# Half of the memory's keys computed inside the gated scan, its weights in joint chunks, and other due times for the side work, in a two-layer hybrid decoder trunk

## The chip, the cores and the metric

The kernel runs on one core of one Trainium2 chip. The metric is the device time of one execution in microseconds (us): 1093.5 us before the change, the median of three runs (1093.49, 1093.5 and 1094.94).

The core has five engines that matter here: PE (TensorE) multiplies matrices, DVE (VectorE) and ACT (ScalarE) work elementwise, POOL (GpSimd) does a few elementwise operations, and SP (SyncE) issues the transfers. Each runs its own list of instructions in order, and a semaphore holds an instruction back until what it reads is there.

## The reference, cut to what matters

Two layers are applied to 256 tokens of 1024 features, all in float32:

```python
for l in range(2):
    h = rmsnorm(x, norm_mix[l])
    u_ssm, q_lat, kv_lat, k_rope, hg_q, hg_f, hg_i, hg_g, gate_logits = split(h @ w_in[l])
    # s5_mixer: a scan over complex states, then a gated product
    y = gelu(s5_scan(u_ssm))                      # (256, 512)
    z_out, z_gate = split(y @ ssm_w_glu[l], 2)    # (512, 2048) weights
    y_ssm = z_out * sigmoid(z_gate)
    y_mla = mla_mixer(...)                        # 8 heads of causal attention, @ mla_w_o
    y_hg  = hgrn2_mixer(...)                      # gated linear recurrence, @ hg_w_o
    g = sigmoid(gate_logits).reshape(1, 256, 3, 1024)
    merged = g[:, :, 0] * y_ssm + g[:, :, 1] * y_mla + g[:, :, 2] * y_hg
    x = x + merged @ w_out[l]
    # memory cross-attention, 4 heads of 128, over 256 memory rows
    mem_n = rmsnorm(mem, norm_mem[l])
    k, v = split(mem_n @ x_w_kv[l], 2)            # the keys and values of the memory
    q = rmsnorm(x, norm_cross[l]) @ x_w_q[l]
    x = x + softmax(q @ k.T / sqrt(128)) @ v @ x_w_o[l]
    gt, up = split(rmsnorm(x, norm_ffn[l]) @ ffn_w_gate_up[l], 2)
    x = x + (silu(gt) * up) @ ffn_w_down[l]
return rmsnorm(x, norm_final)
```

The keys `k` need the memory and `x_w_kv` alone, not `x`.

## The kernel before, in words

**Products.** Activations lie feature-major (128 features on the partitions, 256 tokens along them). A float32 product is computed as three products of rounded parts: each operand is a high part H and a low part L, and H·H, H·L and L·H are summed (`mm3`, and three calls of `mm` in `projB`). In the rows of the trace such a triple reads `x2` with `wH` and `x1` with `wL`, or a 128x512 `wH` product and a 128x256 `wL` product.

**Weights.** They stream in as `Chunk`s of up to 1 MB. SP issues one transfer for each source of a chunk, into one of three raw buffers (`RB`); a chunk is cut into `Unit`s of 128x1024, and each unit is split by a copy on ACT (L232, `wH<-raw`) and a subtraction on DVE (L221, `wL<-raw,wH`), with four buffers each (`HU`). `pump` splits up to four units ahead of the product that uses them, and loads three chunks beyond that. The order of the chunks is the order in which `build_chunks` makes them. The weights of the gated scan, `ssm_w_glu`, come as eight chunks of 512 KB a layer (mode "one", a unit each), all others that matter here as 1 MB with two units.

**Stages.** In a layer the order is: the input projections and the products that feed the three mixers; then `ORDER`: gates of HGRN2 (`gh`), gates of the attention (`gm`), the output of HGRN2 (`ho`), gates of the scan (`gs`), the output of the attention (`mo`), and the gated scan (`zo`, the function `scan`, for the two halves i = 0, 1 of the features). `scan` computes the gate `zg` and the output `zo` in four PSUM banks, each in two halves of the contraction; DVE multiplies and adds them into the merged activation (`mu`, `Tg`), PE transposes it (`mT`, L1415), and ACT and DVE split it into H and L (`m`). Then come the product with `w_out` (`quad` for four 128-row tiles, then two times `halves`), `drain()`, the keys of the memory `Kc` in two halves (`hv<-ex`), the norm, the queries (`hv<-h`), and the rest of the cross-attention and the FFN. `ex` is the normalised memory, prepared by a task that `scan(0)` starts and whose normalising factor `Rm` is multiplied in at the end.

**The side work and its order.** The S5 scan, HGRN2, the attention and the preparation of the memory are generators. While PE's gate and projection products are written out, `pace()` steps them on a clock of estimated times: the next step of a task comes due `LATS[layer]` microseconds after the last (0.9 in layer 0, 1.7 in layer 1). `drain()` and `until()` step them to the end. The framework's scheduler then orders each engine's list by readiness and priority (`tc.high_priority`), and `keep_in_program_order` pins an instruction where it was written. There are eight PSUM banks, and SBUF slots that are planned by the tiles' lifetimes.

**S5 in layer 0.** `b<-Ush,G` are 32 products of the scan's input, DVE turns them in about 16 operations (`w`, then `X`) into states, and `y<-Cp,X` are the products of the states that follow. Gate products (`gt`) and pieces of attention (`S`, `PT`, `oT`, with `Ssb` on DVE and ACT) lie between.

**The start.** `first(k)` runs before each k of the first product: it makes `h` and squares `xp`; POOL adds the squares (L659, `sq<-sq,sq`). After the product come the column sums `ms` (two products with a vector of ones), the factor R (`row`, L629: two transposes on PE and a copy on ACT), `Ue<-quad,R` on DVE, and `hg_bounds`, some 15 operations of 128x4 elements on DVE; the scheduler had put most of those between the `wL` of the first product.

Of the kernel before, what the change touches and what calls it, by code (L numbers as in the profile page):

```python
# [9 lines left out]
F32 = mybir.dt.float32  # L10
# [4 lines left out]
ALU = mybir.AluOpType  # L15
# [85 lines left out]
SLOTS = dict(t4=23, t2=10, t1=4, tn=8, tk=8, ps=8)  # L101

LEAD = 2
LATS = (0.9, 1.7)
WIDE = 2
HEADS = 3

# [51 lines left out]
def trunk(ctx, tc, A, out, plan):  # L159
# [32 lines left out]
    def bank(name="acc"):  # L192
        return plan.tile(pp, "ps", [128, 512], F32, nm(name))
# [16 lines left out]
    def mm(o, l, r, start=True, stop=True):  # L210
        n = width(r)
        now["pe"] += max(0.12, 0.451e-3 * n) if l.dtype == F32R else 2 * max(0.112, 0.844e-3 * n)
        return PE.matmul(o, l, r, start=start, stop=stop)  # L213
# [4 lines left out]

    def tt(o, a, b, op):
        dve(o)  # L220
        DVE.tensor_tensor(out=o, in0=a, in1=b, op=op)  # L221

    def ts(o, a, s1, s2=None, o0=ALU.mult, o1=None):
        dve(o, 0.55e-3)
# [145 lines left out]
    def wcols(w, k0, nk, c0, ncol, mode="col", parts=None):  # L370
        return Chunk([wap(w, k0, nk, c0, ncol)], nk, ncol, mode, parts)
# [92 lines left out]
    def wide(w, nk, c0):  # L464

        return [wcols(w, k, min(4, nk - k), c0, 512, "row") for k in range(0, nk, 4)]
# [16 lines left out]
    def build_chunks(l):  # L483
        C = {}
        w = A["w_in"][l]
        C["u"] = [wcols(w, 4 * i, 4, O_U, 512, "row") for i in range(2)]
        for name_, o, n in (("hf", O_HF, 2), ("hq", O_HQ, 2), ("hi", O_HI, 2), ("hg", O_HG, 2), ("ql", O_QL, 2)):
            if name_ == "hi":
                C[name_] = wide(w, 8, o)
            else:  # L490
                C[name_] = [wcols(w, 0, 8, o + 256 * i, 256) for i in range(n)]
        C["kv"] = wcols(w, 0, 8, O_KV, 256)
        C["kr"] = wcols(w, 0, 8, O_KR, 32, "hl")
        C["uq"] = [wcols(A["mla_w_uq"][l], 0, 4, 384 * i, 384, parts=[
            lambda r: r.rearrange("p k (h d) -> p k h d", d=96)[:, :, :, 0:64],
            lambda r: r.rearrange("p k (h d) -> p k h d", d=96)[:, :, :, 64:96]]) for i in range(2)]
        C["ukv"] = wcols(A["mla_w_ukv"][l], 0, 2, 0, 1024, parts=[
            lambda r: r.rearrange("p k (h d) -> p k h d", d=128)[:, :, :, 0:64],
            lambda r: r.rearrange("p k (h d) -> p k h d", d=128)[:, :, :, 64:128]])
        C["gt"] = {}  # L500
        for part in ORDER:
            for i in range(2):
                if part[0] == "g":
                    C["gt"][part[1], i] = wide(w, 8, O_GT + 1024 * "smh".index(part[1]) + 512 * i)
                elif part == "zo":
                    for k in (0, 2):
                        for n, c0 in (("zg", 1024), ("zo", 0)):
                            C[n, i, k] = wcols(A["ssm_w_glu"][l], k, 2, c0 + 512 * i, 512, "one")
                else:
                    C[part, i] = wide(A[dict(ho="hg_w_o", mo="mla_w_o")[part]][l], 4, 512 * i)  # L510
        C["wo"] = [wcols(A["w_out"][l], 4 * i, 4, 0, 512, "row") for i in range(2)]
        C["wo"] += [wcols(A["w_out"][l], 0, 8, 256 * i, 256) for i in range(2, 4)]
        C["xk"] = [wcols(A["x_w_kv"][l], 0, 8, 256 * i, 256) for i in range(2)]
        C["xq"] = [wcols(A["x_w_q"][l], 0, 8, 256 * i, 256) for i in range(2)]
        C["xv"] = wide(A["x_w_kv"][l], 8, 512)
        C["xo"] = [wcols(A["x_w_o"][l], 0, 4, 512 * i, 512, "col" if i else "row") for i in range(2)]
        w = A["ffn_w_gate_up"][l]
        C["gu"] = [[Chunk([wap(w, 4 * i, 4, 0, 256), wap(w, 4 * i, 4, DFF, 256)], 4, 512, "row") for i in range(2)]]
        C["gu"] += [(wcols(w, 0, 8, 256 * i, 256), wcols(w, 0, 8, DFF + 256 * i, 256)) for i in range(1, 11)]
        C["dn"] = [wide(A["ffn_w_down"][l], KF, 0)] if l == L - 1 else []  # L520
        C["dn"] += [[wcols(A["ffn_w_down"][l], k0, nk, 256 * i, 256, "row" if l == L - 1 else "col")
                     for k0, nk in ((0, 8), (8, 8), (16, 6))] for i in range(2 if l == L - 1 else 0, 4)]
        return C
# [50 lines left out]
    def fold(s, E=None):  # L574

        if E is not None:
            E.tensor_tensor(out=s[:, 0], in0=s[:, 0], in1=s[:, 1], op=ALU.add)
        else:
            tt(s[:, 0], s[:, 0], s[:, 1], ALU.add)
        return s[:, 0]  # L580

    def col_sums(s, ps=None):

        ps = ps if ps is not None else bank("ms")[:, 0:2]
        for tt_ in range(2):
            mm(ps[:, tt_:tt_ + 1], s[:, tt_ * 128:tt_ * 128 + 128], ones)
        return ps

    def hidden(name):
# [52 lines left out]
    def first(k):  # L642

        j = k // 2
        if k == 0:

            warm = bank("warm")
            for q in range(WARM):
                PE.matmul(warm[:, 128 * (q % 4):128 * (q % 4) + 128], still, still, start=True, stop=True)
            now["pe"] = 0.0  # L650
        if k % 2 == 0:
            for o in range(2):
                split_g(nrm.x[k + o][:, 0], nrm.x[k + o][:, 1], xk(k + o), gain("norm_mix", k + o))
        else:
            s = t2([2, 256], F32, "sq")
            act(s, xp[j], AF.Square)
            sq0.append(s)
            if j:
                POOL.tensor_tensor(out=sq0[0], in0=sq0[0], in1=s, op=ALU.add)  # L659
            if j == 3:  # L660
                fold(sq0[0], POOL)


    hb = const.tile([128, 2, 2, 4], F32, name="hb")
# [4 lines left out]
    def hg_bounds():  # L669
        lbp = tn([2, 4])  # L670
        lo = off["hg_lb"]
        lmx = tn([4])
        tt(lmx, gcol[:, lo:lo + 4], gcol[:, lo + 4:lo + 8], ALU.max)
        for l in range(2):
            tt(lbp[:, l, :], gcol[:, lo + 4 * l:lo + 4 * l + 4], lmx, ALU.subtract)
        act(lbp, lbp, AF.Exp)
# [509 lines left out]
    def layer(l, nrm):  # L1186
# [20 lines left out]
            return a  # L1207

        qp = quad(C["u"], hx, first if l == 0 else None, 512 if wider else 256)
        if l == 0:  # L1210
            nrm.sums = col_sums(sq0[0][:, 0])
        ms, r = nrm.finish()
        R = const.tile([128, 256], F32, tag="R", name=nm("R"))
        row_of(r, R)
# [174 lines left out]
        def scan(i):  # L1389
            zg, zo = [[bank(n) for _ in range(2)] for n in ("zg", "zo")]  # L1390

            def half(n, ps, k):
                for tt_ in range(2):
                    projB(C[n, i, k], range(2), 0, 512, ps[tt_], yHL, tt_, kbase=k, first=k == 0, last=k == 2)
            half("zg", zg, 0)
            half("zo", zo, 0)
            if i == 0:
# [4 lines left out]
            for tt_ in range(2):  # L1402
# [2 lines left out]
                ts(g_, g_, 0.25, 0.25, ALU.mult, ALU.add)  # L1405
                stt(u2[tt_], u2[tt_], 1.0, g_, ALU.add, ALU.mult)
            half("zo", zo, 2)
            tps = [bank("mT") for _ in range(2)]
            for tt_ in range(2):
                acc = Tg["h", i][:, tt_]  # L1410
# [8 lines left out]
                    k = 4 * i + 2 * q + o  # L1419
                    split(mx_[k][:, 0], mx_[k][:, 1], two(tps[q])[:, o])  # L1420

        ex = []
        for part in ORDER:
            if part == "zo":
                until(yHL)
# [19 lines left out]
            upd(i, halves(C["wo"][i], mx_), 0.5)  # L1445

        drain()
        Kc = t4([4, 256], F32, "Kc")
        Rm = t1([256], F32, "Rm")
        row_of(rmc, Rm)  # L1450
        for i in range(2):
            kc = Kc[:, 2 * i:2 * i + 2]
            add_up(kc, halves(C["xk"][i], ex))
            tt(kc, kc, Rm.unsqueeze(1).to_broadcast([128, 2, 256]), ALU.mult)
        ms, r = nrm.finish()
        csc = const.tile([128, 4], F32, tag="csc", name=nm("csc"))
        scl, nscl = csc[:, 0:2], csc[:, 2:4]
# [191 lines left out]
```

## Time and profile before

| | |
|---|---|
| time, median of three runs | 1093.5 us |
| the profiled execution's own time | 1094.6 us |
| its span, first to last instruction | 1092.8 us |
| mean granted clock of PE | 0.992 |
| PE busy | 1072.5 us, 98% |
| DVE busy | 829.1 us, 76% |
| ACT busy | 636.4 us, 58% |
| POOL busy | 37.7 us, 3% |

The profiled execution took 1.8 us more than its span, and 1.1 us more than the median. PE is busy for all but about 20 us; DVE and ACT wait often, which costs nothing where PE does not wait for them. The granted clock is in parts of full speed (2.4 GHz); the lower level is 0.50 (1.2 GHz).

### The profile page before, as it was taken

What the parts mean: (1) busy time and instruction counts of PE and PEld (TensorE: products, weight loads), DVE (VectorE), ACT (ScalarE), POOL (GpSimd) and SP (SyncE); (2) the same over time, 40 slices, a digit from 0 to 9 for tenths busy, and PEclk for the clock granted to TensorE, in tenths of its full rate; (3) what the DMA queues carried; (4) which work ended last, traced back from release to release, by engine and by line L of the source; (5) the groups of instructions that cost most, each with busy time, mean ns of one, the idle gap of its engine ahead of it and who ended that gap; (6) DMA issues with size and microseconds to landing.
All of it is one profiled execution on the core that took longest, in us unless ns stands there. A gap on an engine that the chain in (4) does not pass through costs nothing.

```text
span 1092.8 us, 16654 instructions
## 1 busy us (share of the span) xinstructions
PE 1072.5 (98%) x6416; PEld 938.0 (86%) x6416; DVE 829.1 (76%) x1438; ACT 636.4 (58%) x1050; POOL 37.7 (3%) x52
## 2 busy tenths in 40 slices
PE   8999999989899999999999999999999999999997
PEld 8999888878688888888888899888888888888887
DVE  7996777786687789986768887767677868887753
ACT  6645756855455566564565447965545566555542
POOL 4001000000000000000010001000000000000000
PEclk9999999989899999999999999999999999999999
DMA  8745552342655455655656442543474535655551
GB/s 292 214 117 178 176 163 82 116 148 85 204 167 181 133 195 193 193 183 183 188 181 186 121 136 78 191 130 108 163 233 148 197 123 167 194 191 193 174 190 61
DMA packets 145024, 179.08 MB, mean 164 GB/s; under 512 B 13553, under 2 KB 108657, under 8 KB 144945
## 3 DMA queue, kind: packets, MB, share of 16 engines
q1 hardware_dynamic: 144512, 177.45, 50.6%
q8 instruction: 50, 0.82, 0.3%
q10 hardware_dynamic: 432, 0.57, 0.2%
q14 instruction: 30, 0.24, 0.1%
HBM read 174.59 MB, written 1.05 MB: 161 GB/s over the span
## 4 chain that ended last, share of the span: by engine, by line
PE 72%; ACT 1%; DVE 0%; issue 0%; POOLq 0%; POOL 0%; ACTq 0%
PE hv L213 32%; PE dn L213 11%; PE quad L213 6%; PE gt L213 6%; PE xv L213 2%; PE ho L213 1%; PE mo L213 1%; PE lv L213 1%; PE vps L213 1%; PE zg L213 1%; PE y L213 1%; PE zo L213 1%; PE xo L213 1%; PE b L213 1%; PE xS L213 1%; PE q L213 1%
## 5 line engine op out<-in xcount | busy, mean ns | idle before, releaser
L232 ACT ACTIVATE wH<-raw 128x1024 fp32r<-128x1024 f32 (+2 forms) x332 | 340.7, 1032 | 312.7 <-PE hv L213 81.3
L221 DVE TENSOR_TENSOR wL<-raw,wH 128x1024 fp32r<-128x1024 f32 (+2 forms) x332 | 394.8, 1192 | 158.2 <-ACT wH L232 152.1
L213 PE MATMUL hv<-h,wH 128*128 128x512 f32 x848 | 298.2, 396 | 0.0
L213 PE MATMUL hv<-h,wL 128*128 128x256 f32 x848 | 236.8, 282 | 0.0
L213 PEld LDWEIGHTS hv<-h,wH 128*128 128x128 f32 x848 | 158.6, 188 | 35.3 <-issue 0.2
L213 PEld LDWEIGHTS hv<-h,wL 128*128 128x128 f32 x848 | 160.4, 189 | 1.0
L213 PE MATMUL gt<-wH,h 128*128 128x512 f32 x384 | 123.6, 402 | 0.0
L213 PEld LDWEIGHTS gt<-wH,h 128*128 128x128 f32 x384 | 70.7, 188 | 13.4
L213 PE MATMUL gt<-wL,h 128*128 128x512 f32 x192 | 75.2, 397 | 0.2 <-DVE wL L221 0.2
L213 PE MATMUL dn<-dx,wH 128*128 128x512 f32 x176 | 61.6, 394 | 0.0
L213 PE MATMUL dn<-wH,dx 128*128 128x256 f32 (+1 forms) x264 | 58.7, 319 | 0.0
L213 PE MATMUL acc<-h,wH 128*128 128x256 f32 x288 | 52.5, 284 | 0.0
L213 PE MATMUL dn<-dx,wL 128*128 128x256 f32 x176 | 49.3, 280 | 0.0
L213 PEld LDWEIGHTS dn<-wH,dx 128*128 128x128 f32 x264 | 43.6, 189 | 4.0
L213 PE MATMUL quad<-h,wH 128*128 128x512 f32 (+1 forms) x160 | 44.6, 359 | 0.5 <-ACT wH L232 0.5
L213 PEld LDWEIGHTS acc<-h,wH 128*128 128x128 f32 x288 | 44.9, 192 | 0.1
L213 PEld LDWEIGHTS gt<-wL,h 128*128 128x128 f32 x192 | 35.9, 188 | 7.5 <-DVE wL L221 0.3
L213 PE MATMUL dn<-wL,dx 128*128 128x256 f32 (+1 forms) x132 | 41.9, 319 | 0.0
L213 PE MATMUL acc<-h,wL 128*128 128x256 f32 x144 | 40.8, 284 | 0.2 <-DVE wL L221 0.2
L213 PEld LDWEIGHTS dn<-dx,wH 128*128 128x128 f32 x176 | 33.1, 188 | 7.7
L213 PE MATMUL quad<-h,wL 128*128 128x256 f32 x128 | 33.8, 292 | 2.3 <-DVE wL L221 2.1
L213 PEld LDWEIGHTS dn<-dx,wL 128*128 128x128 f32 x176 | 33.1, 188 | 0.0
(375 smaller groups left out, 2017.4 us busy)
## 6 DMA issues: line engine op xcount, KB each, us to landing
raw<-in_w_in_dram SPq DMA_DIRECT2D x48, 1024.0 KB, 5.2
raw<-in_ffn_w_gate_up_dram SPq DMA_DIRECT2D x40, 1024.0 KB, 5.1
raw<-in_ffn_w_down_dram SPq DMA_DIRECT2D x17, 1024.0 KB, 5.2
raw<-in_ssm_w_glu_dram SPq DMA_DIRECT2D x16, 512.0 KB, 3.9
raw<-in_w_out_dram SPq DMA_DIRECT2D x8, 1024.0 KB, 7.3
raw<-in_x_w_kv_dram SPq DMA_DIRECT2D x8, 1024.0 KB, 5.1
raw<-in_ffn_w_down_dram SPq DMA_DIRECT2D x6, 768.0 KB, 4.8
raw<-in_hg_w_o_dram SPq DMA_DIRECT2D x4, 1024.0 KB, 5.1
```

What stands on the lines that cost most here:

```text
L213: return PE.matmul(o, l, r, start=start, stop=stop)
L221: DVE.tensor_tensor(out=o, in0=a, in1=b, op=op)
L232: return ACT.activation(out=o, in_=a, func=f, **kw)
```

## The change

1. **Keys.** `keys(i)` is a new function with what was written behind `w_out`: products `hv<-ex`, two sums, the multiplication with `Rm`. `keys(0)` is called in `scan(1)`, behind the last half of `zo` and a `drain()`, and ahead of the transposes; `keys(1)` stays behind `w_out`. Its chunk `xk` 0 is loaded ahead of those of `w_out`.
2. **Joint chunks.** Gate and output columns of `ssm_w_glu` share a chunk: two sources of 512 KB, one raw buffer of 1 MB, two units. Three raw buffers now hold six units of the scan instead of three.
3. **Due times.** `LATS[0]` goes from 0.9 to 0.7. Steps of the tasks of layer 0 come due earlier; products of tasks and of gates interleave differently in the whole layer.
4. **The start.** The sums `ms` are written in `first(7)` and pinned there, and the first operation of `hg_bounds` is pinned where it is written, behind `Ue`; the others depend on it.

```diff
-LATS = (0.9, 1.7)
+LATS = (0.7, 1.7)
...
     def tt(o, a, b, op):
         dve(o)
-        DVE.tensor_tensor(out=o, in0=a, in1=b, op=op)
+        return DVE.tensor_tensor(out=o, in0=a, in1=b, op=op)
...
                 elif part == "zo":
                     for k in (0, 2):
-                        for n, c0 in (("zg", 1024), ("zo", 0)):
-                            C[n, i, k] = wcols(A["ssm_w_glu"][l], k, 2, c0 + 512 * i, 512, "one")
+                        C[part, i, k] = Chunk([wap(A["ssm_w_glu"][l], k, 2, c0 + 512 * i, 512) for c0 in (1024, 0)], 2, 1024)
...
+        C["xk"] = [wcols(A["x_w_kv"][l], 0, 8, 0, 256)]
         C["wo"] = [wcols(A["w_out"][l], 4 * i, 4, 0, 512, "row") for i in range(2)]
         C["wo"] += [wcols(A["w_out"][l], 0, 8, 256 * i, 256) for i in range(2, 4)]
-        C["xk"] = [wcols(A["x_w_kv"][l], 0, 8, 256 * i, 256) for i in range(2)]
+        C["xk"].append(wcols(A["x_w_kv"][l], 0, 8, 256, 256))
...
-    def col_sums(s, ps=None):
+    def col_sums(s, ps=None, pin=False):
...
-            mm(ps[:, tt_:tt_ + 1], s[:, tt_ * 128:tt_ * 128 + 128], ones)
+            m = mm(ps[:, tt_:tt_ + 1], s[:, tt_ * 128:tt_ * 128 + 128], ones)
+            if pin:
+                tc.keep_in_program_order(m)
...
             if j == 3:
                 fold(sq0[0], POOL)
+                nrm.sums = col_sums(sq0[0][:, 0], pin=True)
...
-        tt(lmx, gcol[:, lo:lo + 4], gcol[:, lo + 4:lo + 8], ALU.max)
+        tc.keep_in_program_order(tt(lmx, gcol[:, lo:lo + 4], gcol[:, lo + 4:lo + 8], ALU.max))
...
-        if l == 0:
-            nrm.sums = col_sums(sq0[0][:, 0])
...
             half("zo", zo, 2)
+            if i == 1:
+                drain()
+                keys(0)
             tps = [bank("mT") for _ in range(2)]
...
+        def keys(i):
+
+            hs = halves(C["xk"][i], ex)
+            if i == 0:
+                Kc.extend((t4([4, 256], F32, "Kc"), t1([256], F32, "Rm")))
+                row_of(rmc, Kc[1])
+            kc = Kc[0][:, 2 * i:2 * i + 2]
+            add_up(kc, hs)
+            tt(kc, kc, Kc[1].unsqueeze(1).to_broadcast([128, 2, 256]), ALU.mult)
...
-        Kc = t4([4, 256], F32, "Kc")
-        Rm = t1([256], F32, "Rm")
-        row_of(rmc, Rm)
-        for i in range(2):
-            kc = Kc[:, 2 * i:2 * i + 2]
-            add_up(kc, halves(C["xk"][i], ex))
-            tt(kc, kc, Rm.unsqueeze(1).to_broadcast([128, 2, 256]), ALU.mult)
+        keys(1)
+        Kc = Kc[0]
```

Three places of the instruction lists, of before and of after. In names as `gt468_2500` the numbers only tell tiles apart.

PE, layer 0, S5: before, the rows ahead of the first product of the states of the second half, `y502<-Cp489,X492`:

```order
L213 MATMUL gt450_2409<-wH451_2410,h14_117 128x512 x2
L213 MATMUL gt450_2409<-wL452_2411,h14_117 128x512
L213 MATMUL y502_2647<-Tm463_2463,Ush49_333 64x4x32
L213 MATMUL S507_2683<-Kh209_1295,Qh207_1293 128x128
L213 MATMUL S507_2683<-Kh209_1295,Qh207_1293 128x256
L213 MATMUL S494_2620<-Kh209_1295,Qh207_1293 128x128
L213 MATMUL S494_2620<-Kh209_1295,Qh207_1293 128x256
L213 MATMUL oT487_2587<-PT486_2585,Vp212_1304 128x256
L213 MATMUL oT487_2587<-PT486_2585,Vp213_1305 128x128
L213 MATMUL y502_2647<-Cp489_2599,X492_2613 64x4x32
```

After, the rows ahead of the same product, now `y503<-Cp484,X493`:

```order
L213 MATMUL gt468_2500<-wH470_2502,h14_117 128x512 x2
L213 MATMUL gt468_2500<-wL471_2503,h14_117 128x512
L213 MATMUL gt469_2501<-wH470_2502,h14_117 128x512 x2
L213 MATMUL gt469_2501<-wL471_2503,h14_117 128x512
L213 MATMUL y503_2654<-Tm455_2419,Ush49_333 64x4x32
L213 MATMUL y503_2654<-Cp484_2562,X493_2598 64x4x32
L213 MATMUL S504_2679<-Kh210_1279,Qh208_1277 128x128
L213 MATMUL S504_2679<-Kh210_1279,Qh208_1277 128x256
L1097 MATMUL PT495_2611<-ident_98,Ssb473_2512 128x128
```

Between the last `b` and this product PE's list had 7 gate triples before and has 18 after; what was left of the attention's `S`, `PT` and `oT` went among them.

DVE at the same place, before: the end of the chain of S5 operations that begins with `w<-cs,b` and ends with `X`:

```order
L1119 TENSOR_REDUCE s479_2552<-Ssb478_2551 128x1
L931 SCALAR_TENSOR_TENSOR w475_2531<-rt436_2346,w473_2529 128x512
L221 TENSOR_TENSOR wL484_2572<-raw416_2279,wH483_2571 128x1024
L221 TENSOR_TENSOR w472_2528<-cs435_2345,w474_2530 128x8x63
L221 TENSOR_TENSOR s480_2556<-s479_2552,lsc203_1283 128x2
L221 TENSOR_TENSOR w473_2529<-sn434_2344,w475_2531 128x8x63
L228 TENSOR_SCALAR Tg488_2596<-Tg488_2596 128x512
L221 TENSOR_TENSOR wL523_2732<-raw416_2279,wH522_2731 128x1024
L228 TENSOR_SCALAR Tg488_2596<-Tg488_2596 128x512
L221 TENSOR_TENSOR X492_2613<-w472_2528,w473_2529 128x8x63
```

And after:

```order
L221 TENSOR_TENSOR wL471_2503<-raw387_2154,wH470_2502 128x1024
L934 SCALAR_TENSOR_TENSOR w465_2483<-rt431_2315,w463_2481 128x512
L228 TENSOR_SCALAR Tg467_2497<-Tg467_2497 128x512
L221 TENSOR_TENSOR w462_2480<-cs430_2314,w464_2482 128x8x63
L1121 TENSOR_REDUCE s474_2513<-Ssb473_2512 128x1
L1122 TENSOR_REDUCE s474_2513<-Ssb473_2512 128x1
L221 TENSOR_TENSOR w463_2481<-sn429_2313,w465_2483 128x8x63
L221 TENSOR_TENSOR wL482_2549<-raw404_2222,wH481_2548 128x1024
L221 TENSOR_TENSOR s475_2517<-s474_2513,lsc204_1267 128x2
L221 TENSOR_TENSOR X493_2598<-w462_2480,w463_2481 128x8x63
```

Before, the chain holds three `wL` and a `mox` (21 rows from the first `w` to `X`), after two `wL` and none (19 rows).

PE, layer 0, the end of the scan's second half, before, where `zo566` is its last product, `mT581` and `mT582` the second half's transposes and `quad` the product with `w_out`:

```order
L213 MATMUL zo566_2938<-wH568_2941,yx513_2701 128x512
L1415 MATMUL mT561_2913<-ident_98,Tg276_1604 128x128 x2
L1415 MATMUL mT562_2914<-ident_98,Tg276_1604 128x128 x2
L213 MATMUL zo566_2938<-wH568_2941,yx513_2701 128x512
L213 MATMUL zo566_2938<-wL569_2942,yx513_2701 128x512
L1415 MATMUL mT581_3024<-ident_98,Tg299_1712 128x128 x2
L1415 MATMUL mT582_3025<-ident_98,Tg299_1712 128x128 x2
L213 MATMUL quad593_3056<-m247_1500,wH571_2959 128x512
L213 MATMUL quad593_3056<-m247_1500,wL572_2960 128x256
L213 MATMUL quad594_3057<-m247_1500,wH571_2959 128x512
L213 MATMUL quad594_3057<-m247_1500,wL572_2960 128x256
```

After, with `zo563` as the last product, and products of the keys, `hv579`, behind it; the transposes `mT558` and `mT559` follow one row below these:

```order
L213 MATMUL zo563_2936<-wH564_2937,yx516_2713 128x512 x2
L213 MATMUL zo563_2936<-wL565_2938,yx516_2713 128x512
L213 MATMUL hv579_3030<-ex557_2905,wL568_2956 128x256
L213 MATMUL hv579_3030<-ex557_2905,wH567_2955 128x512
L213 MATMUL hv579_3030<-ex557_2905,wL568_2956 128x256
L213 MATMUL hv579_3030<-ex571_2983,wH567_2955 128x512
L213 MATMUL hv579_3030<-ex571_2983,wL568_2956 128x256
L213 MATMUL hv579_3030<-ex571_2983,wH567_2955 128x512
L213 MATMUL hv579_3030<-ex571_2983,wL568_2956 128x256
L213 MATMUL hv579_3030<-ex577_3020,wH567_2955 128x512
L213 MATMUL hv579_3030<-ex577_3020,wL568_2956 128x256
L213 MATMUL hv579_3030<-ex577_3020,wH567_2955 128x512
```

The transposes stood directly behind the scan's last product and the `quad` behind them; now the products of the first half of the keys stand there.

PE at the start, a piece of the difference, with `acc` the products that follow the first one and `row` the transposes for R:

```order
@@ -67,5 +67,4 @@
 L213 MATMUL quad20_135<-h14_117,wL31_176 128x256
 L213 MATMUL acc60_376<-h7_110,wH34_213 128x256 x2
-L629 MATMUL row48_325<-ident_98,n46_322 128x128 x2
 L213 MATMUL acc60_376<-h7_110,wL35_214 128x256
 L213 MATMUL acc60_376<-h8_111,wH34_213 128x256 x2
@@ -83,4 +82,5 @@
 L213 MATMUL acc60_376<-h14_117,wH34_213 128x256 x2
 L213 MATMUL acc60_376<-h14_117,wL35_214 128x256
+L631 MATMUL row48_325<-ident_98,n46_322 128x128 x2
 L213 MATMUL acc60_376<-h7_110,wH37_248 128x256 x2
 L213 MATMUL acc60_376<-h7_110,wL38_249 128x256
```

The transposes for R moved behind 15 rows (22 products) of `acc`.

## Rows read from the trace of the kernel before

**Rows 1.** The page's first part: busy time, share and instructions by engine.

```profile
PE 1072.5 (98%) x6416; PEld 938.0 (86%) x6416; DVE 829.1 (76%) x1438; ACT 636.4 (58%) x1050; POOL 37.7 (3%) x52
```

**Rows 2.** PE's waits: total us, how many, the longest.

```profile
PE y L213 <- DVE X L221: 2.5, 1, 2.5
PE mT L1415 <- DVE Tg L221: 2.4, 1, 2.4
PE quad L213 <- DVE wL L221: 2.1, 1, 2.1
PE quad L213 <- DVE m L221: 1.8, 2, 1.5
...
PE PT L1094 <- DVE Ssb L226: 1.0, 1, 1.0
```

**Rows 3.** Windows: busy us of PE, PEld, DVE, ACT, POOL; clock; DMA share; GB/s.

```profile
220.00:240.00 20.00, 16.70 (x119) 13.97 (x119) 17.51 (x35) 9.64 (x20) 0.23 (x2) 0.96 0.57 186
240.00:260.00 20.00, 19.45 (x107) 16.80 (x108) 11.32 (x29) 13.87 (x33) 0.69 (x1) 0.87 0.10 30
280.00:300.00 20.00, 16.18 (x76) 13.11 (x75) 12.11 (x19) 9.23 (x15) 0.00 (x0) 0.83 0.53 175
```

**Rows 4.** Timeline of PE: start, us, operation, idle before and its releaser.

```profile
222.90 3.68 PE L213 MATMUL b<-Ush,G 128*128 128x64 f32 x32
...
238.14 0.57 PE L213 MATMUL y<-Cp,X 128*64 128x128 f32 x2 [2.49 <-DVE X L221]
```

**Rows 5.** The chain of waits: start, us, products in a row.

```profile
391.07 104.25 PE hv L213 x593
...
767.70 5.46 PE gt L213 x24
```

**Rows 6.** Timeline of DVE, the S5 chain's first operation and its `X`.

```profile
224.83 0.69 DVE L221 TENSOR_TENSOR w<-cs,b 128x512 f32<-128x512 f32 x1
...
237.32 0.68 DVE L221 TENSOR_TENSOR X<-w,w 128x504 f32<-128x504 f32 x1
```

**Rows 7.** Timeline of PE at the merge of layer 0.

```profile
287.99 0.66 PE L1415 MATMUL mT<-ident,Tg 128*128 128x128 f32 x4 [2.36 <-DVE Tg L221]
...
290.81 0.77 PE L213 MATMUL quad<-m,wH 128*128 128x512 f32 x1 [1.46 <-DVE m L221]
```

**Rows 8.** Timeline of DVE there.

```profile
287.25 0.69 DVE L221 TENSOR_TENSOR Tg<-Tg,mu 128x512 f32<-128x512 f32 x1
287.85 0.75 DVE L221 TENSOR_TENSOR m<-mT,m 128x256 fp32r<-128x256 f32 x2
288.51 0.68 DVE L221 TENSOR_TENSOR mu<-mu,zo 128x512 f32<-128x512 f32 x1
289.11 1.22 DVE L221 TENSOR_TENSOR wL<-raw,wH 128x1024 fp32r<-128x1024 f32 x1
```

**Rows 9.** Timeline of ACT there.

```profile
280.34 2.01 ACT L232 ACTIVATE wH<-raw 128x1024 fp32r<-128x1024 f32 x2 [3.87 <-DMA raw<-in_w_out_dram]
```

**Rows 10.** Timeline of DVE and of POOL at the start.

```profile
9.13 1.28 DVE L221 TENSOR_TENSOR s<-s 128x4 f32<-128x4 f32 x1
...
12.92 1.30 DVE L228 TENSOR_SCALAR hb<-s 128x4 f32<-128x4 f32 x2
...
8.81 1.58 POOL L659 TENSOR_TENSOR sq<-sq,sq 128x512 f32<-128x512 f32 x1 [5.29 <-ACT sq L232]
...
12.56 1.57 POOL L659 TENSOR_TENSOR sq<-sq,sq 128x512 f32<-128x512 f32 x1 [0.37 <-ACT sq L232]
```

**Rows 11.** Timeline of PE and DVE around R.

```profile
23.64 0.38 PE L629 MATMUL row<-ident,n 128*128 128x128 f32 x2
...
29.99 0.39 PE L213 MATMUL acc<-h,wL 128*128 128x256 f32 x1 [0.23 <-DVE wL L221]
...
24.79 2.23 DVE L221 TENSOR_TENSOR Ue<-quad,R 128x256 f32<-128x256 f32 x4
...
28.72 1.22 DVE L221 TENSOR_TENSOR wL<-raw,wH 128x1024 fp32r<-128x1024 f32 x1
```

**Rows 12.** Timeline of PE and DVE at the first query product.

```profile
327.56 0.39 PE L213 MATMUL hv<-h,wH 128*128 128x512 f32 x1
...
325.48 0.49 DVE L217 SCALAR_TENSOR_TENSOR h<-xp,gcol,h 128x256 fp32r<-128x256 f32 x1
```

More of the change, by code (lines that the diff above doesn't have):

```diff
@@ L1393, in half @@
                 for tt_ in range(2):
-                    projB(C[n, i, k], range(2), 0, 512, ps[tt_], yHL, tt_, kbase=k, first=k == 0, last=k == 2)
+                    projB(C["zo", i, k], range(2), 512 * (n == "zo"), 512, ps[tt_], yHL, tt_, kbase=k, first=k == 0, last=k == 2)
             half("zg", zg, 0)
@@ L1420, in scan @@
                     split(mx_[k][:, 0], mx_[k][:, 1], two(tps[q])[:, o])
-        ex = []
+        ex, Kc = [], []
+        def keys(i):
[6 more added lines that the diff above has]
+            tt(kc, kc, Kc[1].unsqueeze(1).to_broadcast([128, 2, 256]), ALU.mult)
         for part in ORDER:
```

## The prediction, made before the changed kernel was run

> **What bounds the kernel now.** I read the page's first part first: PE is busy for 1072.5 of 1092.8 us [rows 1], so no other engine sets the end, and at most some 20 us are to be had from PE's waits, plus what the clock does beside them. The page's cut into slices shows where they lie, so PE's own waits come next [rows 2]: four of them hold 8.8 us. Two belong to the first layer's merge (`mT` for `Tg`, `quad` for `m`), one with its neighbours to S5 (`y` for `X`, `PT` for `Ssb`), one to the start (`quad` for `wL`). The windows [rows 3] place them: between 220 and 260 us PE is idle 3.30 + 0.55 = 3.85 us, between 280 and 300 us 3.82 us. They also show what the waits cost beyond themselves. The granted clock is 0.96, 0.87 and 0.83 there. Missing clock times 20 us is 0.8 + 2.6 = 3.4 us of full-speed time at the first place, 3.4 at the second. The lower level is 0.50, so each place holds some 6.8 us at 1.2 GHz, and each begins just behind the long wait. About 1.4 us of each lies on further idle time (`PT` 1.0 and a little; `quad` 1.46), where half speed loses nothing: 0.7 of the 3.4. So each costs 2.7 us of slow products beside its idle time. Outside such places PE's products follow each other at 0.176 us (104.25 / 593) and a gate triple takes 0.68 us (5.46 / 8) [rows 5]; these are my prices.
>
> **S5 in layer 0.** The last `b` ends about 226.4 and the product that needs `X` starts at 238.14 after 2.49 us of idle time [rows 4]. DVE's chain runs from 224.83 to 238.0 [rows 6], 13.2 us. PE had little else: 7 triples. In the new lists it has 18, 12.3 us, and some 2 us of `S`, `PT` and `oT`: 14.3 us from the end of `b`. DVE's chain has one `wL` (1.22, 1.14 with overlap) less, no `mox`, and other small operations among it: 10.5 us by the pitch of its rows [rows 6, 8], from 1.6 us before the end of `b`. So `X` is there some 5 us early. The second `X` needs another 5 us of DVE against 2 us of PE, and keeps about 2.5. The waits go: −3.85, and with the first the slow clock: −2.7. What could be late next are `PT` for its `Ssb` and the attention's output for its `wL`; I charge half the `PT` wait of today, 0.5 [rows 2]. Sum −6.05. The gates that are moved here come from behind; their place is then filled by what waited, and PE's total work is the same.
>
> **The merge of layer 0.** Today DVE ends `Tg` at 287.9 [rows 8]; PE has stood from about 285.6, does the transposes, and stands again for `m`, which a `wL` of 1.22 us delays [rows 7, 8]. The `wL` were late because ACT waited 3.87 us for `w_out` with its raw buffers full of half-sized chunks [rows 9]. Now 30 products of the keys stand behind the last `zo`: 30 × 0.176 = 5.3 us, with eight transposes among them (0.7) and the first two products of `quad`: 6.3 us until the second half's transposes. DVE needs up to there: `mu` twice, `Tg` twice (0.6 each by the starts in rows 8), two `m` (0.3 each), one or two `wL` (1.14), one `Kc` sum (0.33): 4.5 to 5.6 us. So PE does not wait, with 0.7 to spare, less than one `wL`; a swap of one `wL` costs up to 1.2, and I charge 1.0. The joint chunks are what lets these `wL` be early: six units are loaded where three were, and the same bytes go on the same queue. With them −3.82 − 2.7 + 1.0 = −5.5. Without them the sums for the keys would themselves be late, and the wait stays (a rival). In layer 1 the same place shows two waits of 0.3 without slow clock (`quad` for `m` twice in rows 2, 1.8 less 1.5, and one `hv` for `wL`); I take −0.6.
>
> **What the keys leave behind.** They had covered the norm after `w_out`: the last `h` is ready at 326.0 and the first query product starts at 327.56 [rows 12], no wait. Half of the cover, 5.6 us, is gone; but two sums and a multiplication (about 1.3 us of DVE, by the 0.33 of a 256-wide sum) and their `wL` (2.3) leave DVE's list there too, so `h` comes 3 to 4 us earlier. Worked by hand from the order, `h` has slack of at least 2 us in either layer. I take 0; with the cover gone it could cost up to 1.5 in each.
>
> **The start.** PE waits 2.11 us for a `wL` at 14.87 [rows 2]. DVE was held before it: operations of 128x4 take 1.28 and 1.30 us and end just when a POOL sum ends (8.81 + 1.58 = 10.39 and 9.13 + 1.28 = 10.41; 12.56 + 1.57 = 14.13 and 12.92 + 1.30 = 14.22, of which 14.14 is the start of the next) [rows 10]. These operations now run behind `Ue`. But the operation that stands next in DVE's list, a `wL` or an `h`, also reads two tensors from SBUF, and would meet the same POOL sum. So I take the wait as staying: 0, bounds −2.1 and +1.5 (one more POOL sum).
> The Trainium skill's page "SBUF — State Buffer", section "SBUF: two separate sides", says that VectorE and GpSimd share a port pair as an exclusive lock, and that the later of a GpSimd operation and a VectorE operation with two SBUF inputs is fully blocked. The ends in rows 10 agree with it. By that rule it is POOL's sums that cost, not the small operations, and taking these away gains nothing; by a reading without it the 2.1 us would go.
> One thing is added: R. Its transposes stood at 23.64 and now stand behind 15 more rows of `acc`, which take 0.36 us per k: 26.3. ACT's copy follows, so `Ue` (2.23 us) starts at about 27.1 instead of 24.79, ends at 29.2, and the `wL` that today starts at 28.72 starts at about 29.6. PE's wait of 0.23 at 29.99 becomes 1.3 [rows 11]: +1.1. If DVE's small operations fill the gap otherwise, 0; if a second `wL` is held too, +3.
>
> **The due times.** In layer 0 each step of a task comes 0.2 us earlier on the planner's clock. What that does outside S5's second half is not in the trace. From below 0: the steps have their inputs, as nearly all have now. From above: some 40 products of tasks in layer 0 come due before their inputs and PE waits up to 0.2 us at each, 8 us. I take the nearest row, one more wait such as `PT` for `Ssb`, 1.0 [rows 2].
>
> **Sum.** −6.05 − 5.5 − 0.6 + 1.1 + 1.0 = −10.05. The profiled execution took 1094.6 us, 1.8 more than its span; 1094.6 − 10.0 = 1084.6. It stood 1.1 above the median of 1093.5, so against that the forecast is 1083.5 us. Its own range, from the terms that I charged and their bounds, is 1080.5 to 1087.
>
> **Rivals.**
> A: one of the two stalls stays. The keys take two PSUM banks while `zg` and `zo` hold four and `mT` two, all eight; if `mT` or `quad` waits for a bank that a late `mu` or sum frees, PE stands behind the keys as it does now, and the clock falls again. For it: the margin of 0.7 us. Against it: the banks of `zg` are free before. About 5.5 back: 1089.
> B: the start gains too, since no `wL` meets a POOL sum: −2.1, and perhaps 2 more where a wait that was left over vanishes: 1079.5. Against it: the ends in rows 10.
> C: slower. The earlier due steps put task products on PE's list ahead of their inputs, all through layer 0. At 40 × 0.2 = 8 us with two more stretches of slow clock (2 × 2.7) it is +13, against −10: 1096.6. It decides from about 0.25 us per step if the clock stays up. Against it: nearly no task product waits now, and the place where they did gains cover.
> D: no change. Both stalls only move: `PT` for `Ssb` in place of `y` for `X`, the transposes behind the keys in place of those before. 1093.5.
>
> **Chances.** The forecast 0.60, A 0.17, B 0.08, C 0.07, D 0.08. A measurement of this kernel can tell 0.2%, 2.2 us, from no change. Faster by more takes in the forecast, A and B: 0.85; the same D: 0.08; slower C: 0.07. The range that leaves two in ten out goes down to B and up to just behind A: 1079.5 to 1089.5.
>
> **What would show it.** In the changed kernel's windows, around the second half of S5 and around the first merge, PE busy 19.5 or more of 20 and the clock at 1.00; `y` for `X` and `mT` for `Tg` gone from PE's waits. At the start a `quad` wait for `wL` of about 2 us still there, and a wait of `acc` for `wL` over 1 us near 30 us. The mean granted clock near 1.0, against 0.992. I am wrong in the mechanism if the clock still falls to 0.5 in either window, in the size if waits of `PT`, `mo` or `gt` beyond 2 us in sum appear in layer 0.

## The result, and the profile after

The changed kernel took 1082.37 us, the median of four runs (1081.18 to 1082.88), against 1093.95 us before (1093.49 to 1094.94, four runs): a ratio of 0.9891, 95% interval 0.9874 to 0.9908, 11.6 us faster. The forecast was 1083.5 us, with a range of 1079.5 to 1089.5. The profiled execution of the changed kernel took 1081.18 us, 1.2 less than its median, so the two profiled executions lie 13.4 us apart, 1.8 more than the medians.

The page's first part, which answers to [rows 1]:

```profile
PE 1064.2 (99%) x6416; PEld 932.7 (86%) x6416; DVE 826.6 (77%) x1438; ACT 639.3 (59%) x1052; POOL 35.6 (3%) x52
```

The records of products are the same 6416, but PE's busy time fell by 8.3 us: products at the lower clock take nearly twice as long (before, a `quad` pair at the merge takes 0.64 us at 293 us and 0.36 us at 297 us), and these stretches are gone. PE's waits (total us, how many, the longest), which answer to [rows 2]:

```profile
PE quad L213 <- DVE wL L221: 2.0, 2, 1.2
PE acc L213 <- DVE wL L221: 1.1, 1, 1.1
...
PE xS L213 <- DVE n L228: 1.0, 1, 1.0
PE ho L213 <- ACT hox L232: 0.9, 1, 0.9
...
PE mo L213 <- DVE Ssb L221: 0.6, 1, 0.6
PE ho L213 <- DVE hox L221: 0.6, 1, 0.6
```

`y` for `X`, `mT` for `Tg` and `quad` for `m` are gone. New are `xS`, `ho` and `mo`, 3.1 us together (`warm`, `xo` and `o`, left out here, wait as they did before). The windows (columns as in [rows 3]):

```profile
180.00:200.00 20.00, 18.51 (x94) 14.98 (x93) 18.61 (x38) 18.29 (x37) 1.06 (x2) 1.00 0.21 56
220.00:240.00 20.00, 20.00 (x113) 16.38 (x112) 17.26 (x33) 13.12 (x25) 0.92 (x3) 1.00 0.66 216
240.00:260.00 20.00, 19.17 (x98) 15.57 (x97) 11.22 (x23) 10.89 (x24) 0.00 (x0) 1.00 0.21 71
280.00:300.00 20.00, 20.00 (x120) 17.39 (x120) 12.80 (x21) 8.52 (x16) 0.00 (x0) 1.00 0.58 191
```

The S5 stretch has 0.83 us of idle time in place of 3.85 and the merge none in place of 3.82, and the clock is 1.00 in both. Three marks on PE cut the difference of the two spans into parts: the first product of the values `vps` (47.13 us before, 45.90 after), the first `xo` of layer 0 (355.94 and 343.96) and the end (1092.8 and 1079.4). The start gave 1.23 us, the rest of layer 0 up to `xo` 10.75, all behind it 1.42.

### The profile page after: what moved, and what is told of

Its sections match the earlier page's. It is cut to its first block, busy times and chain, and to the rows that moved or that the text cites. A ratio compares the mean times of both kernels' runs of the same rounds, so it can differ in the third digit from the quotient of the medians.

```text
span 1079.4 us, 16647 instructions
## 1 busy us (share of the span) xinstructions
PE 1064.2 (99%) x6416; PEld 932.7 (86%) x6416; DVE 826.6 (77%) x1438; ACT 639.3 (59%) x1052; POOL 35.6 (3%) x52
## 4 chain that ended last, share of the span: by engine, by line
PE 75%; ACT 1%; DVE 0%; issue 0%; POOLq 0%; POOL 0%; ACTq 0%
PE hv L213 33%; PE dn L213 11%; PE quad L213 6%; PE gt L213 6%; PE zo L213 2%; PE zg L213 2%; PE xv L213 2%; PE mo L213 1%; PE ho L213 1%; PE lv L213 1%; PE vps L213 1%; PE y L213 1%; PE xo L213 1%; PE xS L213 1%; PE b L213 1%; PE oT L213 1%
```

## The experiments

All are timed against the kernel before, which was run beside them in three groups (e1 to e4, e5 to e8, e9 to e12). Its medians there were 1093.64, 1092.97 and 1092.97; single runs of it spread from 1088.87 to 1096.07. The changed kernel was timed in none of these groups, so differences from its 1082.37 us of about 1 us say little.

**Taking one part back.**

e1: `LATS = (0.9, 1.7)` in the changed kernel.

> The changed kernel with LATS[0] at 0.9 again, all else kept. Theory (the earlier due steps put 18 instead of 7 gate triples between b and the product of the states, and that alone removes the waits of S5): y waits about 2.5 us for X again, the clock falls to 0.5 behind it, 5.5 to 6 us come back, less 1 to 1.5 us of the waits of ho for hox, which go: about 1087 us. Rival (other parts of the change moved the S5 chain too, the joint chunks above all): within 2 us of the changed kernel's 1082.4.

Measured: 1084.49 us (1084.3 to 1085.6), ratio 0.992 [0.9907, 0.9934]. S5's waits are back on PE's timeline as they were:

```profile
236.87 0.40 PE L213 MATMUL y<-Cp,X 128*64 128x128 f32 x2 [2.49 <-DVE X L221]
237.76 0.33 PE L1097 MATMUL PT<-ident,Ssb 128*128 128x128 f32 x1 [0.48 <-ACT Ssb L232]
239.28 0.69 PE L1097 MATMUL PT<-ident,Ssb 128*128 128x128 f32 x2 [1.19 <-DVE Ssb L226]
```

Here the clock cost only half: 0.98 and 0.94 in the windows from 220 and 240 us, so 0.4 + 1.2 = 1.6 us, where before it was 3.4. And the waits of `ho`, `mo` and `xS` are gone. The mechanism was right (the rival, that other parts moved the chain, falls); the price, 2.1 us by the medians, is under the 5 that I expected: the due times take 4.2 us of waits, and 3.3 us of others are there with them that are not there without. With the 1.6 us of clock and 0.4 of smaller waits (`y` for `osb`, `gt` for `wL`) that makes 2.9; the two profiled executions lie 3.1 us apart.

e2: the chunks of `ssm_w_glu` single again.

```diff
-                        C[part, i, k] = Chunk([wap(A["ssm_w_glu"][l], k, 2, c0 + 512 * i, 512) for c0 in (1024, 0)], 2, 1024)
+                        for n, c0 in (("zg", 1024), ("zo", 0)):
+                            C[n, i, k] = wcols(A["ssm_w_glu"][l], k, 2, c0 + 512 * i, 512, "one")
...
```

> The changed kernel with the scan's weights in 512 KB chunks again. Theory (the joint chunks make the splits early enough for the merge): ACT waits for w_out or xk again near 270 to 280 us, PE waits 1 to 4 us in the scan or behind the keys, clock down if it is long: 1084 to 1088 us. Rival (the keys alone cover the merge): 1082.4, within 1 us.

Measured: 1081.1 us (1080.09 to 1083.21), ratio 0.9889 [0.9872, 0.9905]: the joint chunks are worth nothing here. PE waits 0.34 us (`zo`) and 0.50 us (`hv<-ex`) for ACT's `wH`, and in return `xS` does not wait. The keys alone cover the merge: my theory falls, its rival stands.

e3: both halves of the keys behind `w_out` again, with their chunks.

> The changed kernel with both halves of the keys behind w_out again. Theory (the keys stand between Tg and the transposes and cover them): mT waits for Tg and quad for m, 2 to 4 us in sum with 1 to 2.7 us of slow clock: 1085 to 1088 us, and 0.6 more in layer 1. Rival (early weights alone remove the wait): 1082.4 to 1083.4.

Measured: 1086.07 us (1085.91 to 1088.11), ratio 0.9938 [0.9923, 0.9952]. PE's timeline at the merge:

```profile
281.87 0.50 PE L213 MATMUL quad<-m,wH 128*128 128x512 f32 x1 [2.67 <-DVE m L221]
...
283.39 1.11 PE L1415 MATMUL mT<-ident,Tg 128*128 128x128 f32 x4 [0.37 <-DVE Tg L221]
```

3.0 us of waits, nearly all of it at `quad`, and a clock of 0.91 in the window from 280 us (1.8 us) are back, and in layer 1 the two waits of 0.3. Early weights alone do not remove the wait.

e4: the start without the two pins.

> The changed kernel without the two pins at the start. Theory (at the start the change gave 2.1 us, most of it clock, and lost 0.9 to the late R): the single wait of 2.1 us is back with the clock at 0.66 between 15 and 20 us, the wait of acc for wL is back at 0.2, and the first product of v starts 1.2 us later: about 1083.6. Rival (the 2.1 us at the start is what one execution differs from another): 1082.4, or 1081.5 as R is early again.

Measured: 1081.02 us (1080.63 to 1083.44), ratio 0.989 [0.9874, 0.9906]: no slower. In its profile the start is back as expected, one wait of 2.10 us and the clock at 0.66 between 15 and 20 us, the wait of `acc` at 0.24, `vps` at 46.84. But the 0.9 us by which `vps` comes earlier in the changed kernel does not show in the medians, and four runs of this one kernel spread over 2.8 us. The profiled run took 1083.4 us, the other three 1080.6 to 1081.1. What the start does by itself is read from e7 to e9.

**One part alone.**

e5: in the kernel before, the keys and their chunk moved, no more.

> The kernel before with the half of the keys and its chunk moved, nothing else. Theory (the keys alone take the merge's 3.8 us of waits in layer 0 with its slow clock, and 0.6 in layer 1, whatever the chunks are): the waits of y for X, PT and the start's 2.1 us stay, mT for Tg and quad for m go; a wait of up to 1 us for a late weight or for the norm comes: 1093.6 - 5.5 = 1088.1 us, 1087 to 1089. Rival (it needs the joint chunks): 1090 to 1093.

Measured: 1085.28 us (1084.36 to 1085.72), ratio 0.9927 [0.9915, 0.994]. The window of the merge:

```profile
280.00:300.00 20.00, 20.00 (x117) 17.33 (x116) 16.66 (x26) 11.10 (x20) 0.00 (x0) 1.00 0.58 193
```

PE is busy for 20.00 of 20.00 us at clock 1.00, and no wait took the place of the merge's. The gain is 3 us more than expected. About 1 us of that is the wait that I had charged and that did not come. The clock at S5, where nothing was changed, cost 1.6 us in this profile (0.92 from 240 us) where it had cost 3.4, and why is open.

e6: in the kernel before, `LATS = (0.7, 1.7)`, no more.

> The kernel before with LATS[0] at 0.7, nothing else. Theory (the due times alone remove the waits of S5, 3.85 us and up to 3.4 us of clock, and bring the waits of ho for hox and of mo, 2.3 us): merge and start as before, 1093.6 - 4.5 = 1089 us, 1088 to 1090.5. Rival (the gain is as small as the 2.1 us that taking it back cost): 1091.5.

Measured: 1090.11 us (1088.74 to 1092.08), ratio 0.9973 [0.9963, 0.9983]. S5's waits go here as well, but the merge behind them gets worse, as PE's timeline shows:

```profile
282.26 0.50 PE L213 MATMUL quad<-m,wH 128*128 128x512 f32 x1 [3.22 <-DVE m L221]
...
286.48 0.77 PE L213 MATMUL quad<-m,wH 128*128 128x512 f32 x1 [3.05 <-DVE m L221]
```

6.27 us there instead of 3.82. PE comes to the merge earlier, DVE does not: part of the wait taken away at S5 is paid again 50 us later. With the keys in the merge, as in the full change, that is covered. By the medians the due times give 2.9 us alone and cost 2.1 when taken out, the keys 7.7 and 3.7. That the keys cost less to take out than they give alone fits the joint chunks, which e3 kept and which take part of the same stall when the keys are not there (e11): the merge waits 3.0 us with a clock of 0.91 in e3, and 6.27 us with 0.83 in e6, which has neither.

e11: in the kernel before, the joint chunks, no more.

> The kernel before with the joint chunks, nothing else. Theory (after e2: the chunks only bring the weights earlier, which at the merge hides behind the wait for Tg): mT for Tg stays at 2 to 3 us, quad for m falls from 1.5 towards 0.5; 1092 to 1093. My prediction's step (weights late by ACT's wait for w_out are what delays DVE there) as the rival: mT and quad fall together to under 1.5 us, 1089 to 1091.

Measured: 1090.61 us (1087.91 to 1091.86), ratio 0.9981 [0.9968, 0.9994]. At the merge:

```profile
284.41 0.66 PE L1414 MATMUL mT<-ident,Tg 128*128 128x128 f32 x4 [0.74 <-DVE Tg L221]
...
287.23 0.77 PE L213 MATMUL quad<-m,wH 128*128 128x512 f32 x1 [1.46 <-DVE m L221]
```

Neither expectation fits: `mT` waits 0.74 us instead of 2.36, as my prediction's step has it, and `quad` waits 1.46 as before. In this profile early weights take 1.6 us of the stall and about half of its slow clock (0.91 in place of 0.83), which the keys take anyway.

**The start.**

e7: only the 128x4 operations pinned behind `Ue`, the column sums as before.

> The changed kernel with only the 128x4 operations pinned behind Ue; the column sums stand where they stood before. Theory (these are two separate things: the small operations' removal splits the start's wait into 0.7 and 1.2 us and keeps the clock up; the pinned sums only make R late): waits at the start as in the changed kernel, the wait of acc for wL 0.2 instead of 1.1, the first product of v at about 45.0 instead of 45.9: 0.9 us less than the changed kernel, 1080.3 to 1081.5. Rival (the small operations are moved by the sums' pin, or the wait of acc comes from them): 1082.4.

Measured: 1080.28 us (1080.09 to 1080.65), ratio 0.9883 [0.9868, 0.9899]. The start waits 0.73 and 1.21 us at clock 1.00, `acc` waits 0.43 instead of 1.14, `vps` starts at 45.15. The two pins are two things, as expected: in the profiles the one on the small operations brings `vps` forward (46.84 in e4, which has neither), the one on the sums makes R late.

e8: the squares summed on PE, no sums on POOL.

```diff
...
-            if j:
-                POOL.tensor_tensor(out=sq0[0], in0=sq0[0], in1=s, op=ALU.add)
-            if j == 3:
-                fold(sq0[0], POOL)
-                nrm.sums = col_sums(sq0[0][:, 0], pin=True)
...
+            for tt_ in range(2):
+                for j in range(4):
+                    for o in range(2):
+                        mm(ps[:, tt_:tt_ + 1], sq0[j][:, o, tt_ * 128:tt_ * 128 + 128], ones,
+                           start=j + o == 0, stop=j + o == 4)
```

> The changed kernel with the squares of the first norm summed by PE (16 products with the vector of ones instead of 2, none of POOL's four sums), the column sums not pinned. Theory (the wL and h of the start are held by POOL's sums): a wL of 128x512 takes 0.68 and two h 0.9 us between 8 and 16 us, in place of 1.44, 1.91 and 2.38; the waits of quad for wL, 1.96 us, fall below 0.6; R is later by 4 rows, so the wait of acc for wL may stay at 1 to 1.5. First product of acc about 21.3 - 1.4 + 1 (14 products of PE more) = 20.9 us. Rival (the weights' transfers hold the start): durations fall but quad waits as long, now for wH or raw.

Measured: 1076.08 us (1075.67 to 1076.22), ratio 0.9843 [0.983, 0.9857], the fastest of all, 6.3 us below the changed kernel by the medians and 5.2 by the profiled executions. DVE at the start, first of the changed kernel, then of e8:

```profile
9.09 1.44 DVE L221 TENSOR_TENSOR wL<-raw,wH 128x512 fp32r<-128x512 f32 x1 [0.27 <-ACT wH L232]
10.46 1.91 DVE L217 SCALAR_TENSOR_TENSOR h<-xp,gcol,h 128x256 fp32r<-128x256 f32 x2
...
12.89 2.38 DVE L217 SCALAR_TENSOR_TENSOR h<-xp,gcol,h 128x256 fp32r<-128x256 f32 x2
```

```profile
9.16 0.69 DVE L221 TENSOR_TENSOR wL<-raw,wH 128x512 fp32r<-128x512 f32 x1 [0.28 <-ACT wH L232]
9.77 0.88 DVE L217 SCALAR_TENSOR_TENSOR h<-xp,gcol,h 128x256 fp32r<-128x256 f32 x2
...
11.61 0.88 DVE L217 SCALAR_TENSOR_TENSOR h<-xp,gcol,h 128x256 fp32r<-128x256 f32 x2
```

Without POOL's sums the same operations take half the time and less, and `quad` does not wait for `wL` at all. The 14 added products use that up: `acc` starts at 21.46 (21.27 after the change). They cost more than the 1 us that I had charged: a float32 product leaves two records (the 14 raise PE's count from 6416 to 6444), and the sums take 32 records and 3.85 us on PE in place of 4 and 0.50. What the start keeps is the wait of `acc`, 1.14 us, which is gone: `vps` starts at 44.77 in place of 45.90. Up to `xo` come 2.85 us more, behind it 1.2 that were not followed; so most of the gain is not the start. The planner counts these products, its clock stands later, and the interleaving of layer 0 changes: `ho`, `mo`, `zg` and `xS` wait no more (3.3 us), and one `oT` waits 1.18 us. That this comes from the planner's clock was seen in the order, not tested by itself. The granted clock shows no slow stretch up to 1060 us, as in the changed kernel's profile.

e9: the sums on PE in the kernel before, with the small operations where they were, and the planner's clock kept as it was.

> The kernel before with the squares of the first norm summed on PE, as in e8, and the 128x4 operations still between the wL of the start; the rest of the order as before. Theory (POOL's sums hold DVE at the start, whatever operation of two inputs stands there): the 128x4 operations take 0.15 us instead of 1.3, the wait of 2.1 us goes, the clock stays at 1.00 between 15 and 20 us, less 1.4 us for 14 more products: the first product of acc 2 to 2.5 us earlier than the 23.4 of before, or as in e8 21.5; the kernel 1 to 3 us faster, 1090 to 1092. Rival (the small operations hold DVE themselves): they stay at 1.3 us, the wait stays, and the kernel is 1.4 us slower.

Measured: 1092.47 us (1091.68 to 1094.78), ratio 0.9997 [0.9988, 1.0007]. The small operations on DVE's timeline, to be held against the 1.28 and 1.30 of [rows 10]:

```profile
9.12 0.15 DVE L221 TENSOR_TENSOR s<-s 128x4 f32<-128x4 f32 x1
...
10.74 0.23 DVE L228 TENSOR_SCALAR hb<-s 128x4 f32<-128x4 f32 x2
```

The wait of 2.1 us is gone, the clock of the start is 1.00, `acc` starts at 21.57 instead of 23.40 and `vps` 2.25 us earlier. So POOL's sums held DVE, and the rival falls. Between the two profiled executions the gain is there (1092.45 us against 1094.6, with 3.4 us of clock lost at S5 and at the merge in either). Over the medians the kernel is no faster. Most of the 2.25 us is the clock: in e6 and e11 the wait of 2.1 us stands, the clock of the start is 1.00 all the same, and `vps` starts at 45.74 and 45.68, only 0.8 to 0.9 us behind e9. How often the clock fell at the start in the executions without a profile is not on record.

**The clock, and a better version.**

e10: the kernel before with PE filled ahead of `y<-Cp,X`.

```diff
+                if l == 0 and i0 and i == 0:
+                    for _ in range(11):
+                        PE.matmul(o, Ush[:, i0, :], Tm[:, 0, :], start=True, stop=True)
                 mm(o, Ush[:, i0 + i, :], Tm[:, i, :], start=True, stop=False)
```

> The kernel before with 11 products more in S5's second half of layer 0: the first y product is written over and over before it is needed, so PE computes instead of standing in the 2.5 us ahead of y for X (the scheduler puts them among S, PT and oT there). Theory (the slow clock of that place is the price of the standing itself): y for X waits 0 to 0.5 us, the clock of 220 to 260 us is at 1.00 or falls for half as long, and although PE does 2.4 us more, the kernel is 1.5 to 3.4 us faster: 1090 to 1092. Rival (the clock falls there for another reason, or for the PT waits behind it): 1093.5 or more with the clock at 0.96 and 0.87 as before.

Measured: 1090.12 us (1086.42 to 1094.07), ratio 0.998 [0.9966, 0.9993]. The windows around S5:

```profile
220.00:240.00 20.00, 19.33 (x137) 15.84 (x135) 17.50 (x36) 9.64 (x20) 0.23 (x2) 1.00 0.56 181
240.00:260.00 20.00, 19.42 (x117) 16.53 (x117) 11.98 (x29) 13.89 (x33) 0.70 (x1) 1.00 0.08 27
```

With 11 products more the kernel is 2.9 us faster, and the clock stays at 1.00 behind the place. It stays there although `PT` and `oT` still wait 0.67 and 0.58 us between 220 and 260 us, so the rival falls, and the slow clock is a price of the long standing, beside the idle time itself. Of the 2.9 us some comes from elsewhere: the order behind the place moved a little, `mT` waited 1.74 us instead of 2.36, and the clock in the window from 280 us is 0.91 instead of 0.83, 1.6 us.

e12: e8 with the single chunks.

> The kernel of e8 with the scan's weights in 512 KB chunks. Theory (the joint chunks are worth the two waits of 0.3 and 0.5 us for ACT's wH that e2 showed, unless a wait of the norm takes their place): 1076.0 to 1077.2. Rival (the single chunks are the better ones, as the medians of e2 hinted): 1075.0 or less.

Measured: 1076.35 us (1076.2 to 1076.45), ratio 0.9851 [0.9839, 0.9864], 0.3 above e8. It shows no wait for a weight in the merge. With the keys there, the joint chunks are worth 0.3 us by the medians, and e2 showed nothing for them.

## Why the prediction was right, point by point

The forecast was 1.1 us from the median, and the mechanism of the two large terms is shown. Some terms were wrong in size. The terms were priced from the profiled execution, and from profile to profile the change is −13.4 us against −10.05 forecast: −5.7 (S5), −6.5 (the merge), −1.4 (behind the first `xo`), +1.0 (`xS`), +1.1 (due times) and −1.2 (the start) are −12.7 of it. The larger errors went the same way, and that only 1.1 us of them is left in the median is partly luck: the two profiled executions lie 1.8 us further apart than the medians. Of the signs named, one was missed: between 240 and 260 us PE is busy for 19.17 us and not 19.5.

- **S5, −6.05.** Right. In the profile −3.85 of waits [rows 2, 3], +0.83 of new ones (`mo` 0.65, `zg` 0.18; 0.5 charged), −2.7 of clock: −5.7. The first `X` ended at 229.4 and was used at 233.81, 4.4 us early (5 forecast); the second at 234.5 and 236.48, 2.0 early (2.5 forecast). DVE's `X` and the products of PE that use them, without a wait:

```profile
228.75 0.68 DVE L221 TENSOR_TENSOR X<-w,w 128x504 f32<-128x504 f32 x1
233.81 0.38 PE L213 MATMUL y<-Cp,X 128*64 128x128 f32 x2
...
233.84 0.68 DVE L221 TENSOR_TENSOR X<-w,w 128x504 f32<-128x504 f32 x1
236.48 0.43 PE L213 MATMUL y<-Cp,X 128*64 128x128 f32 x2
```

  e1 and e6 show that the due times do it.
- **The merge, −5.5.** Right in the keys (e3, e5), −6.5 measured since no wait at all was left of the 1.0 that I charged. The slow clock before did not begin "just behind the long wait" here: the `quad` product at 288.84 still takes 0.39 us, and those from 290.81 on, behind the second wait, 0.63 to 0.77; the price of 2.7 does not change by it. Wrong was the step "the joint chunks are what lets these `wL` be early", without which "the wait stays": without them the wait does not stay (e2, e12). Alone they take 1.6 us of the stall (e11); beside the keys they are redundant.
- **Layer 1, −0.6.** The two waits went (e3 has them again), and what lies behind the first `xo` gave 1.42 us in all. The other 0.8 shows no wait, but it comes with the keys as well: from that `xo` to the end it is 736.9 us before, 735.4 in e5, where the keys alone are moved, and 736.7 in e3.
- **What the keys leave behind, 0.** Wrong in size: `xS` waits for the norm in layer 0, on PE's timeline:

```profile
325.43 0.50 PE L213 MATMUL ms<-ones,sq 128*128 128x1 f32 x4
326.92 1.10 PE L213 MATMUL xS<-Kc,Qc 128*128 128x256 f32 x4 [0.99 <-DVE n L228]
```

  I had followed `h` [rows 12], which had slack. What came late is the norm's factor `n`: it stood behind a `wL` of 1.23 us and a sum on DVE (325.21 to 326.7). My bound of 1.5 holds it.
- **The due times elsewhere, +1.0.** `ho` waits 1.49 us for `hox`; two waits of before (0.27 and 0.15) went: +1.1.
- **The start, 0 for the wait and +1.1 for R.** R was right: the wait of `acc` grew from 0.23 [rows 11] to 1.14, and e7 takes most of it away with the pin (0.43). The step "So I take the wait as staying: 0" was right in the waiting and wrong in the time. PE waits 1.96 of the 2.11 us, but in two pieces. First the kernel before, then the changed one, each with its window of 15 to 20 us (columns as in [rows 3]):

```profile
14.87 0.74 PE L213 MATMUL quad<-h,wL 128*128 128x256 f32 x4 [2.11 <-DVE wL L221]
15.00:20.00 5.00, 4.86 (x28) 4.61 (x29) 3.95 (x9) 2.73 (x4) 0.41 (x1) 0.66 1.06 365
```

```profile
13.02 0.74 PE L213 MATMUL quad<-h,wL 128*128 128x256 f32 x4 [0.74 <-DVE wL L221]
15.93 0.75 PE L213 MATMUL quad<-h,wL 128*128 128x256 f32 x4 [1.22 <-DVE wL L221]
15.00:20.00 5.00, 4.07 (x34) 4.07 (x35) 4.46 (x11) 2.73 (x4) 0.00 (x0) 1.00 1.08 369
```

  The clock, 0.66 between 15 and 20 us before, stays at 1.00. That is 1.7 us, and the first product ended 2.13 us earlier. The sum had charged the clock at S5 and at the merge, and had left it out here. It is no firm gain: of the six profiles with the single wait of 2.1 us the clock falls in four (before, e4, e5, e10) and stays at 1.00 in two (e6, e11); in the five with two pieces it never falls. Against the `vps` of e6 and e11, 45.74 and 45.68, the changed kernel's 45.90 is no gain at all.
  The Trainium skill's page "SBUF — State Buffer", section "SBUF: two separate sides", has VectorE and GpSimd locking each other out of a port pair. The runs agree: with POOL's sums on, small operations, `wL` or `h` are held alike, with them off none is (e8, e9). `hb`, which reads one tensor, was held too (1.30 us for two in [rows 10], 0.23 in e9); the case of two inputs that the prediction quotes does not cover it.

Rival A did not come: no product waits for a bank behind the keys. B's time did not come, since the `wL` and `h` do meet POOL's sums. C's mechanism shows at `ho`, at 1.5 us and not 13. D is out: both stalls are gone, and what replaced them is 3.1 us.

## What to carry to other kernels

Where PE stands for a chain of another engine, work that needs neither can take the stall away without a faster chain (which was not tried here): the keys were there anyway and took 6.5 us. Price such a stall with the slow clock that can follow, and look whether the time saved is paid again at the next stall behind it, as in e6. An operation of 128x4 elements that takes 1.3 us is waiting for something: find out for what before moving it.

## What the runs showed of the hardware

**The clock can fall while PE is busy.** In e2 and e4 (not in the profile of the changed kernel) it was at 0.50 from about 176 to 179.5 us, in S5's first half. The windows of e4:

```profile
164.00:174.00 10.00, 10.00 (x61) 8.39 (x60) 9.97 (x14) 6.61 (x12) 0.22 (x2) 1.00 0.30 91
174.00:182.00 8.00, 8.00 (x61) 7.85 (x60) 1.63 (x3) 1.23 (x3) 1.64 (x1) 0.79 0.46 151
```

PE is busy throughout by these rows, first with sixteen records of 128x1, then with the small products of `y`: at 176.25 us two of them take 0.64 us, the same two 0.38 us in the changed kernel. It cost 1.65 us: the product that waits for `hox` starts 138.54 us behind the first `vps` in both, 136.89 in the changed kernel. The profiles of e3, e6 and e7, with the same rows there, do not show it either.

**A kernel's time goes with its mean granted clock.** Of the twelve runs of e10 two took 1086.42 and 1086.60 us with a mean clock of 0.999, three 1093.10 to 1094.07 with 0.993; the kernel before goes from 1088.87 us at 0.998 to 1096.07 at 0.989 in 29 runs. By the windows a single stretch cost 1.6 to 1.8 us or 3.4, at the same place with nearly the same order before it. That such stretches make most of the spread is likely and not shown, since only one execution of each kernel has windows: e7, e8 and e12, without one in their profile, spread over 0.6 us or less in four runs, but the changed kernel, without one either, over 1.7.

**Small sums are not free on PE.** The sixteen products of 128x1 over 128 rows take 3.85 us of PE in e8; POOL's four sums of the same squares take 5.5 us in the changed kernel, and DVE is held beside them. At the start the two come out nearly even: the first `acc` starts at 21.46 us in e8 and at 21.27 in the changed kernel.
